# Differential attention's eight key tiles computed with layer 1's paired tiles, and all ten keys finished there

## The chip, the cores and the metric

The kernel runs on one core of one Trainium2 chip. The metric is the device time of one execution in microseconds (us). The engines are named as the profile names them: PE (TensorE, matmuls; PEld its weight loads), DVE (VectorE), ACT (ScalarE), POOL (GpSimd), SP (SyncE, which here only starts transfers). SBUF and PSUM are the on-chip memories; a "tile" below is a buffer in one of them, and a "column tile" is 128 output columns of a projection.

## The reference, cut to what matters

Two layers over 640 tokens: 512 latent ("sample") and 128 context ("prompt") tokens, 2048 wide. Layer 1 (the odd one) projects the normalised input with one matrix whose columns are split between differential attention (c) and grouped-query attention (d):

```python
p = h @ w_in                            # odd layer: cq, ck, cv, cg, dq, dk, dv, dg
cq = rms_norm(cq, cqn);  ck = rms_norm(ck, ckn)     # 2 maps x 4 heads of 128
q_d = rms_norm(q_d, dqn); k_d = rms_norm(k_d, dkn)  # 8 query heads, 2 key heads
new = (ck, cv, k_d, v_d)                            # context tokens: returned
cq, ck, q_d, k_d = (apply_rope(x, cos, sin) for x in ...)   # latent tokens
ck_all = concatenate([ctx[0], ck]);  cv_all = ...   # 256 cached + 512 latent keys
o1 = attend(cq[:, 0], ck_all[:, 0], cv_all)
o2 = attend(cq[:, 1], ck_all[:, 1], cv_all)
o_c = rms_norm(o1 - lam * o2, c_on) * (1.0 - lam_init)
y = concatenate([merge(o_c) * silu(cg), merge(o_d) * silu(dg)]) @ w_out
```

A key thus needs its projection, an RMS norm over 128 features, a gain, the axial rotation of the latent tokens, and, for the kernel's score products, a layout with the features on the partitions ("columns"). Every float32 product is made of three products of rounded parts (high x high, high x low, low x high); `split` (L296 to L298) makes the parts, the high one on ACT and the low one on DVE.

## The kernel before

**Two ways to project.** `run_tiles` (L388) makes one column tile at a time: 16 blocks of the contraction, 2 halves of 320 tokens, 3 products each, in four quarters of four blocks. Its weights are loaded five quarters ahead on SP's queue and split three quarters ahead. `run_pairs` (L533) makes two column tiles together with seven half-sized products, called M1, M5, M6, M2, M7, M3, M4 in this order, in place of eight (a scheme of Strassen's kind); each has 8 blocks and 3 products on 320 columns. Their operands are sums of weight blocks built on DVE (`operand`), and of the moving operand built beforehand (`forms`). The result of a column tile leaves in two halves through `done`: tile 0 after M2 and M3, tile 1 after M7 and M4.

**Slots.** After each quarter (`run_tiles`) or half product (`run_pairs`) a `slot` lets other work in: every generator of the list `prep` goes on by one yield, the list `attn` by a paced number of steps (`steps` per quarter, half of it between the two token halves), and a `fill` by a rate per quarter. In layer 1's attention stage the fill is `fill1` (L191): four blocks of the adaLN weights times the condition, two DVE products for each of 16 rows of a block, and a fold at its end; 68 steps in all, from the ninth quarter on (FILL1_FROM 8) at FILL1 0.85 a quarter. The tile framework that builds the program works out the waits, and it puts the instructions of each engine in order; this order is not always the written one.

**Layer 1's front** is `project` at L1715: gates, D's keys and all values. The first six column tiles run singly, the other twenty in ten pairs: four of gates, one of D's two keys (`dk`), one of D's values, four of C's. `gate_out` (L1652), `key_out` (L1678) and `value_out` (L1670) take the results out. A value is turned to rows there and stored (`value_rows`); a D key is only stored raw in `kdram` (L1684).

**Layer 1's attention stage** is the `run_tiles` at L1768: 26 single column tiles. First eight `dq` tiles; two of them start one grouped-query attention (`pair_gen`), whose keys are read back raw and finished by `k_gen` (L670) beside the first tile. Then for each of C's four heads two `cq` tiles and two `ck` tiles, then two late gates. For a `ck` tile `k_gen` copies the projection out of PSUM (`stage`), transposes it to rows (five PE transposes), sums the squares (ACT, L694), applies the gain (DVE, L696, L699), takes the power -0.5 (POOL, L704), scales (ACT, L707), rotates (DVE, L714 to L719), finishes the attention in hand (`drain(attn)`), transposes the two blocks of cached keys (L726) and the five blocks of the key back, and splits them into the tiles `k0h`, `k0l` or `k1h`, `k1l`, one buffer each. With the second key `diff_gen` (L1562) starts: 14 steps; a block's two maps go through one score tile `S` in PSUM, each by scores on PE (L847 to L849), the maximum on DVE (L809), its scaling and the exponential on ACT (L811, L816). Attention's pace is 1.6 steps a quarter up to the eleventh tile, then 1.1, and 1.75 in the late gates' tiles.

**What is loaded at the seam.** After the front SP issues the load of `tables` (rotation tables, 768 KB, L1718), then lambda, the output gains, and the cached and raw first key (L679, L684). Temporary tiles of the attention stage share few buffers: `rp` three, `stg` two.

Of the kernel before, what the change touches and what calls it, by code (L numbers as in the profile page):

```python
# [51 lines left out]
FILL1 = 0.85  # L52
# [4 lines left out]
def trunk_kernel(ctx: ExitStack, tc: tile.TileContext, I: dict, O: dict):  # L57
# [286 lines left out]
    prep, attn = [], []  # L344

# [324 lines left out]
    def k_gen(ap, pp, tag, src, gain, new_out, vals=None, then=None):  # L670

        vx = []

        def v_in(j):
            vx.append(ap.tile([P, 5, P], F32, tag="stg", name="vx", bufs=2))
            nc.sync.dma_start(vx[j].rearrange("p b f -> p (b f)"), vals[1][j])

        raw = ap.tile([P, 2, P], F32, tag="ctxk", name="ctxk", bufs=1)
        nc.sync.dma_start(raw, src.rearrange("(c p) d -> p c d", p=P))  # L679
        if isinstance(pp, tuple):  # L680
            x = stage(ap, pp)
        else:
            x = ap.tile([P, NT], F32, tag="stg", name="kx", bufs=2)
            nc.sync.dma_start(x, pp)  # L684
        if vals:
            v_in(0)
        yield
        ss = small.tile([P, 5], F32, tag="ss", name="ss")
        kg = ap.tile([P, 5, P], F32, tag="rp", name="kg", bufs=3)
        junk = ap.tile([P, P * st["sets"]], BF16, tag="junk", name="junk", bufs=1)[:, 0:P]  # L690
# [9 lines left out]
        if vals:  # L700
            v_in(1)
# [3 lines left out]
        yield  # L705
# [3 lines left out]
        m1 = ap.tile([P, 4, P], F32, tag="rp", name="m1", bufs=3)  # L709
        m2 = ap.tile([P, 4, P], F32, tag="rp", name="m2", bufs=3)  # L710
        x = kg[:, 0:4, :].rearrange("p b (a h f) -> p (b a) h f", a=2, h=2)
        y = m1.rearrange("p b (a h f) -> p (b a) h f", a=2, h=2)
        z = m2.rearrange("p b (a h f) -> p (b a) h f", a=2, h=2)
        V.tensor_mul(y, x, cosR[:, :, None, :].to_broadcast([P, 8, 2, 32]))  # L714
        yield
        V.scalar_tensor_tensor(out=z[:, :, 0, :], in0=x[:, :, 1, :], scalar=-1.0, in1=sinR,
                               op0=ALU.mult, op1=ALU.mult)
        V.tensor_mul(z[:, :, 1, :], x[:, :, 0, :], sinR)
        V.tensor_add(m1, m1, m2)  # L719
        yield  # L720
        drain(attn)
# [5 lines left out]
        split(hi[:, 0:CTX], lo[:, 0:CTX], t[:, 0:CTX])  # L727
        t = to_rows(lambda b: kg[:, b, :], False)
# [3 lines left out]
        if vals:  # L732
            yield
            hi, lo = st["v"] = tuple(ap.tile([P, 7, 2 * P], F32R, tag=t, name=t) for t in ("vh", "vl"))
            ctx_v(ap, vals[0], hi, lo, 2 * P)
            for j in range(2):
                cols = slice(j * P, (j + 1) * P)
                split(hi[:, 2:7, cols], lo[:, 2:7, cols], vx[j])
        if then:
            attn.append(then())  # L740
# [133 lines left out]
    def pair_gen(ap, width, k, v, qs, banded, begin, emit, done, sinks):  # L874
# [38 lines left out]
        for u in range(7):  # L913
# [8 lines left out]
            if u < 5:  # L922
                score(u, 1)
# [959 lines left out]
```

## Time and profile before

| what | value |
|---|---|
| runs shown | 2266.32 us median (2265.68 to 2266.66, 3 runs) |
| profiled execution | 2267.87 us, its span 2265.9 us |
| mean granted PE clock | 0.996 |
| layer 1's pairs | about 1190 to 1436 us |
| layer 1's attention stage | about 1436 to 2005 us |
| output projection of layer 1 | from about 2005 us |

The profile is one execution taken by the hardware profiler. Times in its rows count from the span's start; durations of groups are means in ns. "busy" of an engine is the time covered by its instructions. A group's row ends with the idle time of the engine just before these instructions and what ended it. Matmuls overlap, so their cost is read from the distance of their starts and not from their duration. SPq is SP's queue of transfers. L numbers are lines of the kernel before.

### The profile page before, as it was taken

What the parts mean: (1) busy time and instruction counts of PE and PEld (TensorE: products, weight loads), DVE (VectorE), ACT (ScalarE), POOL (GpSimd) and SP (SyncE); (2) the same over time, 40 slices, a digit from 0 to 9 for tenths busy, and PEclk for the clock granted to TensorE, in tenths of its full rate; (3) what the DMA queues carried; (4) which work ended last, traced back from release to release, by engine and by line L of the source; (5) the groups of instructions that cost most, each with busy time, mean ns of one, the idle gap of its engine ahead of it and who ended that gap; (6) DMA issues with size and microseconds to landing.
All of it is one profiled execution on the core that took longest, in us unless ns stands there. A gap on an engine that the chain in (4) does not pass through costs nothing.

```text
span 2265.9 us, 41110 instructions
## 1 busy us (share of the span) xinstructions
PE 2221.5 (98%) x15660; PEld 2148.4 (95%) x15660; DVE 1693.1 (75%) x2981; ACT 1167.9 (52%) x2473; POOL 223.5 (10%) x341
## 2 busy tenths in 40 slices
PE   7999999999999999999999999999999999999999
PEld 5889999999999999999999999899999999999999
DVE  4659898988888978877876666585766786576765
ACT  4335554645344445444744445577775666664443
POOL 2221101000100100000200000100001111111010
PEclk9999999999999999999999999999999999999999
DMA  9985556565453426753763333432424343246541
GB/s 357 330 287 173 160 167 198 173 188 161 154 156 113 150 85 219 218 148 106 261 200 108 117 110 112 151 103 70 124 84 140 96 132 111 83 134 224 166 135 45
DMA packets 377189, 354.03 MB, mean 156 GB/s; under 512 B 17170, under 2 KB 324848, under 8 KB 376480
## 3 DMA queue, kind: packets, MB, share of 16 engines
q1 hardware_dynamic: 360272, 291.07, 42.1%
q0 software_dynamic: 15856, 58.11, 7.3%
q8 instruction: 123, 2.02, 0.4%
q10 hardware_dynamic: 864, 2.23, 0.3%
q14 instruction: 74, 0.61, 0.1%
HBM read 307.17 MB, written 44.17 MB: 155 GB/s over the span
## 4 chain that ended last, share of the span: by engine, by line
PE 83%; DMA 4%; issue 4%; ACT 3%; DVE 3%; POOL 1%; SPq 1%; POOLq 0%; DVEq 0%; ACTq 0%
PE pq L626 10%; PE pq L628 10%; PE pq L627 10%; PE pa L332 6%; PE pa L333 6%; PE pb L332 6%; PE pa L334 6%; PE pb L333 6%; PE pb L334 6%; PE T L835 2%; PE S L847 2%; PE S L849 1%; PE S L848 1%; PE T L178 1%; DMA ada<-in_ada_w 1%
## 5 line engine op out<-in xcount | busy, mean ns | idle before, releaser
L297 ACT ACTIVATE wh<-raw 128x512 fp32r<-128x512 f32 (+1 forms) x388 | 233.2, 602 | 343.4 <-PE pb L333 227.4
L332 PE MATMUL pa<-h,wh 128*128 128x320 f32 x1152 | 367.7, 319 | 0.6 <-DVE sum L425 0.4
L332 PE MATMUL pb<-h,wh 128*128 128x320 f32 x1152 | 360.4, 313 | 0.9 <-ACT h L297 0.9
L333 PE MATMUL pa<-h,wh 128*128 128x320 f32 x1152 | 359.4, 312 | 0.9 <-DVE h L298 0.9
L334 PE MATMUL pa<-h,wl 128*128 128x320 f32 x1152 | 358.3, 311 | 0.0
L333 PE MATMUL pb<-h,wh 128*128 128x320 f32 x1152 | 357.8, 311 | 0.0
L334 PE MATMUL pb<-h,wl 128*128 128x320 f32 x1152 | 357.8, 311 | 0.0
L298 DVE TENSOR_TENSOR wl<-raw,wh 128x512 fp32r<-128x512 f32 (+1 forms) x388 | 253.5, 654 | 110.7 <-ACT wh L297 99.7
L626 PE MATMUL pq<-h,wh 128*128 128x320 f32 x960 | 297.7, 310 | 0.0
L627 PE MATMUL pq<-h,wh 128*128 128x320 f32 x960 | 296.6, 309 | 0.0
L628 PE MATMUL pq<-h,wl 128*128 128x320 f32 x960 | 296.4, 309 | 0.0
L332 PEld LDWEIGHTS pa<-h,wh 128*128 128x128 f32 x1152 | 217.4, 189 | 13.8 <-issue 12.5
L626 PE MATMUL pq<-T,wh 128*128 128x320 f32 x720 | 223.3, 310 | 0.0
L333 PEld LDWEIGHTS pa<-h,wh 128*128 128x128 f32 x1152 | 217.6, 189 | 5.9 <-issue 4.5
L628 PE MATMUL pq<-T,wl 128*128 128x320 f32 x720 | 222.6, 309 | 0.3 <-DVE wl L298 0.3
L627 PE MATMUL pq<-T,wh 128*128 128x320 f32 x720 | 222.4, 309 | 0.0
L332 PEld LDWEIGHTS pb<-h,wh 128*128 128x128 f32 x1152 | 217.2, 189 | 2.1 <-ACT h L297 1.1
L334 PEld LDWEIGHTS pa<-h,wl 128*128 128x128 f32 x1152 | 217.2, 189 | 2.1 <-issue 2.1
L333 PEld LDWEIGHTS pb<-h,wh 128*128 128x128 f32 x1152 | 217.5, 189 | 0.0
L334 PEld LDWEIGHTS pb<-h,wl 128*128 128x128 f32 x1152 | 217.2, 189 | 0.2 <-DVE wl L298 0.2
L297 ACT ACTIVATE wh<-sx 128x512 fp32r<-128x512 f32 x180 | 112.7, 632 | 154.5 <-PE pq L627 106.5
L251 DVE SCALAR_TENSOR_TENSOR acc<-adaw,sT,acc 128x1024 f32<-128x1024 f32 x150 | 189.3, 1278 | 0.0
(389 smaller groups left out, 4782.4 us busy)
## 6 DMA issues: line engine op xcount, KB each, us to landing
adaw<-in_ada_w SPq DMA_DIRECT2D x80, 512.0 KB, 3.9
raw<-in_od_w_in SPq DMA_DIRECT2D x148, 256.0 KB, 3.0
raw<-in_ev_w_in SPq DMA_DIRECT2D x130, 256.0 KB, 3.4
ada<-in_ada_w SPq DMA_DIRECT2D x11, 2048.0 KB, 12.7
adaw<-in_ada_w SPq DMA_DIRECT2D x64, 256.0 KB, 2.7
w<-in_od_w_in SPq DMA_DIRECT2D x30, 512.0 KB, 3.9
w<-in_ev_w_in SPq DMA_DIRECT2D x27, 512.0 KB, 3.7
adah<-in_ada_w SPq DMA_DIRECT2D x20, 512.0 KB, 9.2
```

Of the source, the lines that this page charges most:

```text
L178: PE.matmul(acc[32 * g:32 * g + 32, 0:wd], sT[:, kt, :], w[:, kt % m, :], start=(i < 4), stop=(i >= KT - 4), tile_position=(0, 32 * g))
L251: V.scalar_tensor_tensor(out=acc[c], in0=w, scalar=sT[:, kt, c:c + 1], in1=acc[c], op0=ALU.mult, op1=ALU.add)
L297: A.activation(hi, x, AF.Copy)
L298: V.tensor_sub(lo, x, hi)
L332: PE.matmul(ps, wh[:, i, :], hi[:, sl], start=(j == js[0] if alone else (pos == 0 and j == 0)), stop=False)
L333: PE.matmul(ps, wh[:, i, :], lo[:, sl], start=False, stop=False)
L334: PE.matmul(ps, wl[:, i, :], hi[:, sl], start=False, stop=(j == js[1] - 1 if alone else (pos == 3 and j == 3)))
L626: PE.matmul(ps, wh[:, j, :], hi, start=(first and h == 0 and j == 0), stop=False, skip_group_check=True)
L627: PE.matmul(ps, wh[:, j, :], lo, start=False, stop=False, skip_group_check=True)
L628: PE.matmul(ps, wl[:, j, :], hi, start=False, stop=(final and h == 1 and j == 3), skip_group_check=True)
L835: PE.transpose(t[:, i * P:(i + 1) * P], p, ident)
L847: PE.matmul(d, q[0][:, bs], k[0][:, ks], start=True, stop=False)
```

## The change

The eight `ck` column tiles leave the attention stage's list and join the front as four more pairs, behind the pair of D's keys and ahead of the values; the front has 14 pairs, and the attention stage 18 single tiles. All ten keys are finished in the front: a generator `key_chain` for each, with seven parts in the slots, makes the norm, gain and rotation and the transposes back, and stores the key as columns in `kdram` (ten entries now). The halves of the result go into the accumulator tiles `sq` and `acc`; `busy` holds back the next pair's results until the chain that reads the tile is through. The rotation tables for rows are loaded at the first pair into a part of `tables` that is free by then. In the attention stage a key is loaded as columns and only split, after the two transposes of the cached keys. In place of `drain(attn)` two counters (`passed`) tell when the attention in hand has made its last scores, or used its last values. A head's reload is a generator, `head_back`, started with its second query tile.

Sizes and rates: FILL1 0.85 becomes 1.1; steps are 1.6 a quarter up to the ninth tile and 2.0 after it, the late gates' tiles included; `rp` has two buffers in place of three, and a new tag `kk` has one. The first key's loads are issued ahead of the load of `tables`.

```diff
-FILL1 = 0.85
+FILL1 = 1.1
...
+    passed = {"scores": 0, "values": 0}
...
-    def k_gen(ap, pp, tag, src, gain, new_out, vals=None, then=None):
...
+    def key_rows(x, ss, kg, junk, gain):
+
         for sample in (True, False):
             t = to_rows(cols_of(x), sample)
             for i, b in enumerate(range(4) if sample else (4,)):
...
+        return r
+
+    def key_scale(kg, r, new_out, m1, cos):
+
         for b in range(5):
             A.activation(kg[:, b, :], kg[:, b, :], AF.Copy, scale=r[:, b:b + 1])
         nc.gpsimd.dma_start(new_out, kg[:, 4, :])
...
+    def key_turn(kg, m1, m2, sin):
...
+    def new_keys(ap, tag, raw):
+
         hi, lo = (ap.tile([P, 896], F32R, tag=tag + t, name=tag + t) for t in "hl")
         st[tag] = (hi, lo)
         t = psT()
         for c in range(2):
             PE.transpose(t[:, c * P:(c + 1) * P], raw[:, c, :], ident)
         split(hi[:, 0:CTX], lo[:, 0:CTX], t[:, 0:CTX])
+        return hi, lo
...
+            if u == 4:
+                passed["scores"] += 1
...
+    def key_chain(j, t):
+        yield
+        x, (gain, new_out) = st[t], KEYS[j][1:3]
+        ss = small.tile([P, 5], F32, tag="ss", name="ss")
+        kg = xr_tile("kg").rearrange("p (b f) -> p b f", b=5)
+        junk = pS.tile([P, 1024], F32, tag="S", name="sqj")[:, 0:P]
+        r = key_rows(x, ss, kg, junk, gains[gain])
+        yield
+        yield
+        m1 = x[:, 0:NS].rearrange("p (b f) -> p b f", b=4)
+        key_scale(kg, r, new_out, m1, cosF)
+        yield
+        m2 = xr_tile("m2")
+        key_turn(kg, m1, m2[:, 0:NS].rearrange("p (b f) -> p b f", b=4), sinF)
+        yield
+        yield
+        A.copy(m2[:, SPLIT], to_rows(lambda b: kg[:, b, :], False))
+        A.copy(m2[:, 0:NS], to_rows(lambda b: m1[:, b, :], True))
+        nc.gpsimd.dma_start(kdram[j], m2)
+        busy.discard(t)
...
     def key_out(j):
-        x = xr_tile("kx")
-
         def put(t, sl, src):
-            A.copy(x[:, sl], src)
+            A.copy(st[t][:, sl], src)
             if (j, "k") in half_done:
-                nc.gpsimd.dma_start(kdram[j], x)
+                busy.add(t)
+                prep.append(key_chain(j, t))
             half_done.add((j, "k"))
...
     def front_done(p, t, h, src):
-        outs[t](("sq", "acc")[t], HV[h][1], src)
+        tag = ("sq", "acc")[t]
+        while tag in busy:
+            advance(prep, len(prep))
+        outs[t](tag, HV[h][1], src)
...
-    nc.sync.dma_start(tables, I["k_tables"])
     close("mid")
     open_pool("odd")
+    st["sets"], st["rp"] = 2, 2
...
+    def key_load(j, tag, bufs):
+        ap = pools["cur"]
+        raw = ctx_keys(ap, KEYS[j][3])
+        x = ap.tile([P, NT], F32, tag=tag, name="kx", bufs=bufs)
+        nc.sync.dma_start(x, kdram[j])
+        return raw, x
+
+    def key_split(tag, raw, x):
+        hi, lo = new_keys(pools["cur"], tag, raw)
+        split(hi[:, CTX:], lo[:, CTX:], x)
+
+    first = key_load(0, "stg", 2)
+    nc.sync.dma_start(tables, I["k_tables"])
     odd_start()
...
+    def wait_for(what, n):
+        while passed[what] < n:
+            advance(attn, 1)
+
+    def head_back(h, n):
+        ap = pools["cur"]
+        k = key_load(2 + 2 * h, "kk", 1)
+        yield
+        yield
+        wait_for("scores", n)
+        key_split("k0", *k)
+        k = key_load(3 + 2 * h, "kk", 1)
+        craw = ap.tile([P, 2, 2 * P], F32, tag="ctxv", name="ctxv", bufs=1)
+        nc.sync.dma_start(craw, I["cache_c_v"][0, 0, h].rearrange("(c p) d -> p c d", p=P))
+        yield
+        key_split("k1", *k)
+        vx = [ap.tile([P, 5, P], F32, tag="stg", name="vx", bufs=2) for _ in range(2)]
+        for j in range(2):
+            nc.sync.dma_start(vx[j].rearrange("p b f -> p (b f)"), vdram[2 * h + j])
+        yield
+        wait_for("values", n)
+        hi, lo = st["v"] = tuple(ap.tile([P, 7, 2 * P], F32R, tag=t, name=t) for t in ("vh", "vl"))
+        split(hi[:, 0:2, :], lo[:, 0:2, :], craw)
+        for j in range(2):
+            cols = slice(j * P, (j + 1) * P)
+            split(hi[:, 2:7, cols], lo[:, 2:7, cols], vx[j])
+        attn.append(diff_then(h)())
...
     for h in range(4):
-        for m in range(2):
-            jobs.append((OD["cq"] + (m * 4 + h) * P, q_job(f"q{m}", "c_q_norm")))
-        for m in range(2):
-            more = (None, diff_then(h)) if m else ((I["cache_c_v"][0, 0, h], vdram[2 * h:2 * h + 2]),)
-            jobs.append((OD["ck"] + (m * 4 + h) * P,
-                         k_job(f"k{m}", I["cache_c_k"][0, 0, m, h], "c_k_norm", O["new_c_k"][0, 0, m, h], *more)))
-
-    brisk = {len(jobs): 1.75, len(jobs) + 1: 1.75}
-    brisk.update((i, 1.6 if i < 11 else 1.1) for i in range(2, len(jobs)))
+        jobs.append((OD["cq"] + h * P, q_job("q0", "c_q_norm")))
+        jobs.append((OD["cq"] + (4 + h) * P, last_q(h)))
+
+    brisk = {len(jobs): 2.0, len(jobs) + 1: 2.0}
+    brisk.update((i, 1.6 if i < 9 else 2.0) for i in range(2, len(jobs)))
```

More of the change, by code (lines that the diff above doesn't have):

```diff
@@ L752, in q_gen @@
         yield
[L753 removed]
+        m = ap.tile([P, NS], F32, tag="rp", name="qm", bufs=st["rp"])
         V.tensor_mul(m, x[:, 0:NS], cosT)
@@ new lines, in last_q, with f @@
+    def last_q(h):
+        def f(pp):
+            g = q_gen(pools["cur"], pp, "q1", gains["c_q_norm"])
+            next(g)
+            back = head_back(h, banded_before + 4 + h)
+            next(back)
+            prep.append(g)
+            prep.append(back)
+        return f
+    banded_before = passed["scores"]
+    for h in range(4):
+        jobs.append((OD["cq"] + h * P, q_job("q0", "c_q_norm")))
+        jobs.append((OD["cq"] + (4 + h) * P, last_q(h)))
+    brisk = {len(jobs): 2.0, len(jobs) + 1: 2.0}
```

121 lines of the change are left out of this document (59 added, 62 removed).

## The prediction

> **What bounds the kernel now.** I read the page first: engine totals, then the chain of work that ended last.
>
> ```profile
> PE 2221.5 (98%) x15660; PEld 2148.4 (95%) x15660; DVE 1693.1 (75%) x2981; ACT 1167.9 (52%) x2473; POOL 223.5 (10%) x341
> ...
> PE 83%; DMA 4%; issue 4%; ACT 3%; DVE 3%; POOL 1%; SPq 1%; POOLq 0%; DVEq 0%; ACTq 0%
> ```
>
> TensorE is the bound in total and on the chain, so a change in its work counts in full unless another engine takes its place. Totals hide stages, so next come the busy times by stretch: layer 1's pairs from 1190 to 1436 us, its attention stage from 1436 to 2005, and in it 200 us of differential attention. Columns: length, then PE, PEld, DVE, ACT, POOL, clock, DMA share, GB/s.
>
> ```profile
> 1190.00:1436.00 246.00, 246.00 (x1692) 245.77 (x1691) 159.64 (x235) 120.01 (x232) 16.16 (x30) 1.00 0.37 113
> 1436.00:2005.00 569.00, 557.23 (x3903) 533.43 (x3902) 390.60 (x739) 373.89 (x894) 65.04 (x91) 1.00 0.36 110
> 1700.00:1900.00 200.00, 196.50 (x1383) 188.79 (x1382) 151.44 (x293) 119.41 (x317) 27.93 (x45) 1.00 0.41 123
> ```
>
> In the pairs TensorE never stops, and VectorE is at 65%, ScalarE at 49%. In the attention stage TensorE stops for 2%. VectorE is at 69% there and at 76% in the differential part: it is the engine to watch.
>
> **The change part by part.**
>
> *Fewer products.* The duration of a matmul row (0.31 us) overlaps the next one, so I go by starts, in a pair and in a single tile.
>
> ```profile
> 1192.80 0.31 PE L627 MATMUL pq<-h,wh 128*128 128x320 f32 x1
> ...
> 1200.87 0.31 PE L628 MATMUL pq<-h,wl 128*128 128x320 f32 x1
> ...
> 1950.54 0.31 PE L332 MATMUL pb<-h,wh 128*128 128x320 f32 x1
> ...
> 1952.15 0.31 PE L334 MATMUL pb<-h,wl 128*128 128x320 f32 x1
> ```
>
> The first two are 55 steps apart (56 products): 8.07 / 55 = 0.1467 us. The last two are 11 apart: 0.1464. A single tile is 2 halves x 16 x 3 = 96 products, so two tiles are 192 and 28.2 us. A pair is 7 forms x 8 x 3 = 168 products and 24.6 us. Four pairs for eight tiles save 4 x 24 x 0.1467 = **14.1 us** of TensorE work, with no condition in the code on it. The ten transposes of each key stay as many; they move to the front with the chain. The two of the cached keys stay behind.
>
> *The start of the attention stage.* The waits of PE there, longest in total first (total, times, longest):
>
> ```profile
> PE S L847 <- ACT p L816: 2.3, 5, 0.6
> PE T L656 <- DMA kx<-kd: 2.2, 1, 2.2
> PE T L656 <- ACT kg L707: 1.5, 2, 1.1
> PE T L656 <- DVE k1l L298: 1.2, 1, 1.2
> ```
>
> and the clock just behind the second:
>
> ```profile
> 1444.00:1446.00 2.00, 0.65 (x4) 0.68 (x5) 0.80 (x4) 0.20 (x1) 0.00 (x0) 0.85 1.05 377
> 1446.00:1448.00 2.00, 2.00 (x9) 2.00 (x9) 0.36 (x1) 1.35 (x6) 0.00 (x0) 0.50 0.87 335
> 1448.00:1450.00 2.00, 2.00 (x13) 2.00 (x13) 1.50 (x4) 1.63 (x7) 0.68 (x2) 0.80 0.23 70
> ```
>
> The first D key comes back raw, behind the 768 KB of tables on SP's queue. Its transposes hold TensorE for 2.2 us, and the lost clock (0.15 + 0.50 + 0.20 of 2 us) is 1.7 us more. After, the key comes back as columns, ahead of the tables on that queue, and only the cached key's two transposes (128 KB) can hold TensorE; waits on the scaled key (1.5 us, L707) leave the stage. The gain lies between 0, if the cached key is as late as the raw one was, and 2.2 + 1.7 + 1.5 = 5.4. I take the middle, rounded down: **2.5 us**. [...]
>
> *The key chain in the front.* What a key costs VectorE and ScalarE (count | busy, mean ns):
>
> ```profile
> L714 DVE TENSOR_TENSOR m<-kg,tables 128x512 f32<-128x512 f32 x10 | 6.9, 693 | 18.9 <-ACT kg L707 18.9
> L696 DVE TENSOR_TENSOR kg<-T,gain_rows 128x512 f32<-128x512 f32 x10 | 6.9, 690 | 6.1 <-ACT junk L694 6.1
> L719 DVE TENSOR_TENSOR m<-m,m 128x512 f32<-128x512 f32 x10 | 6.9, 689 | 0.2
> ...
> L716 DVE SCALAR_TENSOR_TENSOR m<-kg,tables 128x256 f32<-128x256 f32 x10 | 4.2, 419 | 0.0
> L718 DVE TENSOR_TENSOR m<-kg,tables 128x256 f32<-128x256 f32 x10 | 4.2, 419 | 0.0
> ...
> L707 ACT ACTIVATE kg<-kg,r 128x128 f32<-128x128 f32 x50 | 15.9, 391 | 15.1 <-POOL r L704 15.1
> ...
> L694 ACT ACTIVATE junk<-T 128x128 bf16<-128x128 f32 x50 | 13.9, 277 | 2.9 <-PE T L656 1.7
> ...
> L694 ACT ACTIVATION_READ_ACCUMULATOR junk<-T 128x1 f32 x50 | 9.7, 195 | 0.0
> ```
>
> VectorE: 2.9 us in these rows, about 3.2 with the one product of 128 columns. ScalarE: 5 x (0.391 + 0.277 + 0.195) = 4.3 us, and about 0.9 for the two copies that gather the columns (an estimate by size from the same rows). A pair of keys adds 6.4 and 10.4 us of records. With 65% and 49% of 24.6 us as the base, less the gate's or the value's own work, VectorE comes to some 21 us and ScalarE to some 21 us of 24.6: near 85%. Each chain must end before its accumulator is written again ten slots of 1.76 us later (17.6 us); it needs, from its rows and with 1.2 us for POOL's power, about 12 us. Can a pair live with such a load? The nearest row is in layer 0's pairs:
>
> ```profile
> 740.00:780.00 40.00, 39.66 (x271) 39.40 (x270) 39.12 (x65) 16.76 (x29) 4.85 (x9) 1.00 0.48 146
> ```
>
> VectorE at 98% cost TensorE 0.3 us of 40. Five key pairs are 123 us, so that rate gives 1.0 us. ScalarE was low there, so both engines loaded at once isn't shown; the other end is a late chain, 3 us in each pair (17.6 against 12 and half as much again in queues), 15 us. I take **1 us**. POOL and SP's extra transfers (eight keys out and eight back, 320 KB each) lie beside a DMA share of 0.37.
>
> *A denser differential part.* This is the part that decides.
>
> ```profile
> L211 DVE SCALAR_TENSOR_TENSOR acc<-adaw,sT,acc 128x512 f32<-128x512 f32 x60 | 43.6, 745 | 2.7 <-DMA adaw<-in_ada_w 2.7
> L298 DVE TENSOR_TENSOR wl<-raw,wh 128x512 fp32r<-128x512 f32 x38 | 26.2, 689 | 14.8 <-ACT wh L297 12.1 <-PE T L656 2.2
> ```
>
> These rows are of 1700 to 1900 us: 38 quarter tiles in 200 us, so a head (16 quarters now) lasts 16 x 200 / 38 = 84 us, with 64 us of VectorE. After, a head has 8 quarters: 28.2 us less TensorE and 1.7 less for transposes, so 54 us. VectorE loses 8 splits (5.5 us), two key chains (6.4) and, since the adaLN fill runs at 1.1 rather than 0.85 a quarter on half the quarters, 18.9 - 13.1 = 5.8; records overlap by a tenth, so 16 of the 17.7. That leaves 48 us of 54: **88%, where it was 76%**. ScalarE falls to about 35 of 54. The fill still ends in time: 63 quarters x 1.1 = 69 steps for 68.
>
> The second pressure is latency: attention takes one step per half quarter (12 products, 1.76 us), and a head's two maps share the one score tile.
>
> ```profile
> 1950.36 0.34 PE L849 MATMUL S<-k0h,q0l 128*128 128x384 f32 x1
> ...
> 1950.74 0.96 DVE L809 TENSOR_REDUCE nm<-S 128x1 f32<-128x768 f32 x1 [1.72 <-PE S L849]
> ...
> 1952.06 0.99 ACT L816 ACTIVATE p<-S,nm,rq 128x768 f32<-128x768 f32 x1
> ```
>
> From the last score's step (1950.36 + 0.18) to the end of the exponential is 2.5 us. Now three or four half quarters' worth of products often lie between; after, 1.76 us do: 0.7 us short in 4 wide blocks of 4 heads, 11 us if nothing fills it. What can fill it are later products, which depend only on split weights. Bounds: **below**, the stage loses the share it loses now (3.5 of 200 us), and being 120 us shorter gives back 2.1; **above**, each of the 16 pairs of scores is also held by one pair of adaLN products ahead of the maximum (2 x 0.745): 16 x 2.2 = 35 us, less 2.1. The nearest row for full VectorE is
>
> ```profile
> 1836.00:1856.00 20.00, 20.00 (x138) 19.62 (x137) 19.74 (x37) 11.29 (x27) 2.29 (x3) 1.00 0.44 128
> 1856.00:1876.00 20.00, 19.72 (x143) 18.69 (x142) 18.71 (x35) 12.67 (x32) 2.77 (x5) 1.00 0.37 110
> ```
>
> VectorE at 96% for 40 us, TensorE 0.28 us idle. It speaks for the lower end, but it was a burst and the load after is steady, so I let half of the 11 us stand: 5.5 - 2.1, about **+3.4 us**.
>
> The queue of the waiting instruction: the keys' split waits on VectorE behind the maximum and the fill; behind it stand the weight splits, which are three quarters ahead (some 20 us with attention between), so TensorE feels it late. SP's reload of the second key waits for the first one's split, with weight loads behind it that are five quarters ahead. Both covers cost nothing while they last; gone, a weight load's landing (about 3 us by the page) is open each time.
>
> *Sum* against the profiled execution: span 2265.9 - 14.1 - 2.5 + 1.0 + 3.4 = 2253.7; with the 2.0 us around the span (2267.87 against 2265.9) 2255.7. The median of the runs stands 1.55 below the profiled execution, so **2254.1 us**.
>
> **The rivals.**
>
> *VectorE becomes the bound of the differential part (slower).* Place: between the two maps of each block. For it: 88% load, and a maximum that must pass the fill. [...] Against it: the 0.28 us of the burst above. It decides from the point where the other terms' 15.6 + 2.1 = 17.7 us are used up, 1.1 us a pair of scores. At its full price of 35 us the time is 2266.3 - 15.6 + 33 = 2283.7; at 1.4 us a pair it is 2271.
>
> *The front gives it back (no change).* The chains come late by 3 us in each of five pairs, because ScalarE and VectorE are near 85% at once and the next pair waits for the accumulator: 15 us for 1, so 2268. For it: nothing in the pairs loads both. Against: 17.6 us of room for 12.
>
> *All of it is gain (faster still).* The start gains 5.4, the front costs nothing and the differential part its lower bound: 2266.3 - 14.1 - 5.4 - 2.1 = 2244.7. For it: the burst rows. I count it with the forecast, at the low end.
>
> **How the numbers follow.** Runs of this kernel tell 0.2% (4.5 us) from no change. Forecast and its faster tail, below 2261.8: 0.68. The front, or a middling differential part, between 2261.8 and 2270.8: 0.13. VectorE as the bound, above: 0.19, of which over half ends below 2275. The range 2246 to 2275 leaves about 0.07 below and 0.09 above; the forecast's own is 2246 to 2261.
>
> **What would show it.** *Right:* 96 x 8 fewer products of single tiles and 672 more of pairs; the pairs' stage about 99 us longer with PE still near 100%; no wait of a transpose on `kx` and no half clock at the stage's start; a head of the differential part in 54 to 57 us with VectorE near 88%. *Wrong:* waits of the score products on the exponential (L847 on L816) growing from 2.3 us to over 15; idle PE in the key pairs, on `wl` or on a key's transposes; a new half-clock window at the start on the cached key's load; the fill unfinished when the stage ends, left for the output projection.

## The result and the profile after

| | before | after |
|---|---|---|
| median of the runs | 2266.49 us (2262.49 to 2269.07, 6 runs) | 2258.62 us (2256.06 to 2262.14, 6 runs) |
| ratio | | 0.9967, 95% interval 0.9956 to 0.9978 |
| profiled execution, its span | 2267.87, 2265.9 us | 2262.14, 2260.3 us |

The kernel became faster by 0.33%: 7.5 us, with an interval of 5 to 10. The forecast was 12.2 us less on the span, 2254.1 us for the median; the time lies inside its range. The direction was right, the size was not: about 60% of the gain came.

The page of the kernel after, engine totals and the chain that ended last:

```profile
PE 2212.2 (98%) x15564; PEld 2133.7 (94%) x15564; DVE 1728.9 (76%) x3027; ACT 1190.5 (53%) x2519; POOL 229.7 (10%) x349
...
PE 80%; ACT 6%; DMA 5%; DVE 4%; issue 4%; POOL 2%; SPq 0%; POOLq 0%; ACTq 0%; DVEq 0%
```

TensorE has 96 instructions fewer, the 4 x 24 products of the change. It is still the bound, with 3 points less of the chain. The totals can't say where the missing 40% went. So I cut the two traces at the same places, the first and the last projection products of a stage. PE's timeline of the kernel before (start, duration):

```profile
1180.78 0.31 PE L626 MATMUL pq<-h,wh 128*128 128x320 f32 x1
...
1431.87 0.31 PE L628 MATMUL pq<-T,wl 128*128 128x320 f32 x1
...
1432.02 0.31 PE L332 MATMUL pb<-h,wh 128*128 128x320 f32 x1
...
2131.45 0.31 PE L334 MATMUL pa<-h,wl 128*128 128x320 f32 x1
```

and of the kernel after:

```profile
1182.40 0.31 PE L627 MATMUL pq<-h,wh 128*128 128x320 f32 x1
...
1548.87 0.31 PE L629 MATMUL pq<-T,wl 128*128 128x320 f32 x1
...
1549.01 0.31 PE L332 MATMUL pb<-h,wh 128*128 128x320 f32 x1
...
2126.16 0.31 PE L334 MATMUL pa<-h,wl 128*128 128x320 f32 x1
```

The pairs take 366.5 us in place of 251.1 (+115.4), the single tiles behind them, 26 or 18 of the attention stage and the first 5 of the output projection, 577.1 in place of 699.4 (-122.3). Ahead of the pairs, in code that the change doesn't touch, the two executions differ by 1.6 us; over all fourteen profiled executions of this document the pairs start between 1178.8 and 1185.0 us. The single tiles are cut further at the starts of the third and of the ninth tile. Columns as in the prediction. Before:

```profile
1432.00:1471.30 39.30, 35.34 (x231) 32.88 (x230) 18.71 (x38) 21.75 (x64) 6.98 (x10) 0.96 0.57 183
...
1625.20:2131.50 506.30, 496.71 (x3469) 480.00 (x3468) 349.56 (x661) 299.60 (x724) 61.29 (x97) 1.00 0.42 129
```

After, with the pairs and a stretch of key pairs ahead of them:

```profile
1182.40:1548.90 366.50, 362.71 (x2499) 360.04 (x2498) 255.17 (x390) 204.75 (x490) 40.78 (x66) 1.00 0.35 107
...
1294.00:1434.00 140.00, 136.21 (x942) 133.58 (x942) 105.76 (x171) 93.39 (x275) 26.80 (x40) 1.00 0.32 99
...
1549.00:1579.60 30.60, 30.41 (x211) 29.38 (x210) 12.63 (x24) 15.03 (x32) 3.24 (x4) 1.00 0.75 240
...
1579.60:1734.70 155.10, 151.79 (x1068) 144.44 (x1067) 119.89 (x218) 113.81 (x231) 11.24 (x10) 1.00 0.37 114
...
1734.70:2126.20 391.50, 377.82 (x2621) 357.56 (x2620) 291.21 (x558) 247.54 (x548) 45.68 (x73) 1.00 0.46 144
```

The first two tiles became 8.7 us shorter: PE idles 0.2 us there, before it was 4.0, and the clock is 1.00 for 0.96. The pairs, which had no idle time, now have 3.8 us of it (366.50 - 362.71), all in the 140 us with the key chains. The stretch from the ninth tile on (C's heads, the late gates and the output projection's first tiles) is 114.8 us shorter, and its idle time rose from 9.6 to 13.7 us although it is shorter. The kernel before also loses 1.7 us there to a lower clock (0.63 and 0.52 of full speed from 2090 to 2094 us, in the output projection), the kernel after nothing.

To turn this into the terms of the forecast one more price is needed, that of the 100 transposes (ten for each key) which moved into the pairs. The first experiment gives it: without its stops the front is 360.6 us long, so 360.6 - 251.1 - 672 x 0.1467 = 10.9 us, 0.109 each. I take the same price for them in the attention stage, where none was measured; an error of 0.02 there would shift 2 us (0.02 x 100 transposes) between the terms.

| term | forecast | measured | how |
|---|---|---|---|
| fewer products | -14.1 | -14.1 | 96 fewer x 0.1467 |
| key chains in the front | +1.0 | +5.9 | 115.4 - 98.6 - 10.9 |
| start of the attention stage | -2.5 | -6.5 | -8.7, of it 20 moved transposes 2.2 |
| the rest of it and the output tiles | +3.4 | +7.8 | -113.6 + 768 x 0.1467 + 80 x 0.109 |
| sum | -12.2 | -6.9 | 115.4 - 122.3 |

All three small terms were too small, one with the gain and two with the loss. How well do such cuts repeat? The pairs do to 0.02 us in all executions of one code: 366.5 us in the three profiled kernels whose front is that of the change, 360.6 us in the seven with the first experiment's edit. The single tiles do not: the first experiment's kernel has the code of the change there and takes 575.1 us in place of 577.1, which makes the fourth term +5.3 in place of +7.8. And the profiled execution of the kernel after is the slowest of its six, 3.5 us above their median. So the fourth term is known as 5 to 8 us.

What TensorE waits for, total, times and longest, in the pairs of the kernel after:

```profile
PE T L657 <- DVE sq L703: 2.0, 5, 0.4
PE T L657 <- DVE acc L703: 1.8, 5, 0.4
```

and from the ninth single tile on, after:

```profile
PE S L846 <- ACT p L815: 3.8, 7, 0.8
PE T L657 <- DVE xr L1213: 2.2, 3, 1.7
PE T L1624 <- DVE on L1619: 2.2, 3, 0.7
```

and before, same stretch (the forecast's row, 2.3 us in 5 waits on the exponential, was of another stretch, 1436 to 2005 us):

```profile
PE S L847 <- ACT p L816: 2.4, 3, 1.6
...
PE T L1622 <- DVE on L1617: 0.9, 1, 0.9
```

Ten waits in the pairs, one for each key, are the clearest change. Behind the pairs nothing stands out: 1.4 us more on the exponential, 1.3 on the norm.

### The profile page after: what moved, and what is told of

Same layout as the page of the kernel before. It is cut to its first block, busy times and chain, and to the rows that moved or that the text cites. A ratio compares the mean times of both kernels' runs of the same rounds, so it can differ in the third digit from the quotient of the medians.

```text
span 2260.3 us, 41098 instructions
## 1 busy us (share of the span) xinstructions
PE 2212.2 (98%) x15564; PEld 2133.7 (94%) x15564; DVE 1728.9 (76%) x3027; ACT 1190.5 (53%) x2519; POOL 229.7 (10%) x349
## 4 chain that ended last, share of the span: by engine, by line
PE 80%; ACT 6%; DMA 5%; DVE 4%; issue 4%; POOL 2%; SPq 0%; POOLq 0%; ACTq 0%; DVEq 0%
PE pq L627 11%; PE pq L628 11%; PE pq L629 11%; PE pa L332 5%; PE pa L333 5%; PE pb L332 5%; PE pa L334 5%; PE pb L333 5%; PE pb L334 5%; PE T L834 2%; PE S L846 2%; DMA adaw<-in_ada_w 1%; PE S L848 1%; PE S L847 1%; PE T L178 1%
## 5 line engine op out<-in xcount | busy, mean ns | idle before, releaser
L627 PE MATMUL pq<-h,wh 128*128 128x320 f32 x1088 | 338.1, 311 | 0.0
L628 PE MATMUL pq<-h,wh 128*128 128x320 f32 x1088 | 336.2, 309 | 0.0
L629 PE MATMUL pq<-h,wl 128*128 128x320 f32 x1088 | 335.9, 309 | 0.0
L332 PE MATMUL pa<-h,wh 128*128 128x320 f32 x1024 | 325.2, 318 | 0.5 <-DVE sum L426 0.5
L332 PE MATMUL pb<-h,wh 128*128 128x320 f32 x1024 | 321.5, 315 | 0.9 <-ACT h L297 0.9
L333 PE MATMUL pa<-h,wh 128*128 128x320 f32 x1024 | 319.7, 312 | 0.2 <-DVE h L298 0.2
L333 PE MATMUL pb<-h,wh 128*128 128x320 f32 x1024 | 318.4, 311 | 0.0
L334 PE MATMUL pa<-h,wl 128*128 128x320 f32 x1024 | 317.6, 310 | 0.0
L298 DVE TENSOR_TENSOR wl<-raw,wh 128x512 fp32r<-128x512 f32 (+1 forms) x364 | 236.7, 651 | 87.9 <-ACT wh L297 83.9
L627 PE MATMUL pq<-T,wh 128*128 128x320 f32 x816 | 253.8, 311 | 0.0
L628 PE MATMUL pq<-T,wh 128*128 128x320 f32 x816 | 252.0, 309 | 0.0
L627 PEld LDWEIGHTS pq<-h,wh 128*128 128x128 f32 x1088 | 204.3, 188 | 0.8 <-issue 0.8
L332 PEld LDWEIGHTS pa<-h,wh 128*128 128x128 f32 x1024 | 192.5, 188 | 13.2 <-issue 12.2
L628 PEld LDWEIGHTS pq<-h,wh 128*128 128x128 f32 x1088 | 204.4, 188 | 0.0
L629 PEld LDWEIGHTS pq<-h,wl 128*128 128x128 f32 x1088 | 204.2, 188 | 0.0
L333 PEld LDWEIGHTS pa<-h,wh 128*128 128x128 f32 x1024 | 192.6, 188 | 5.9 <-issue 5.4
L332 PEld LDWEIGHTS pb<-h,wh 128*128 128x128 f32 x1024 | 193.5, 189 | 2.6 <-ACT h L297 1.1
```

Of the source, the lines that this page charges most:

```text
L298: V.tensor_sub(lo, x, hi)
L332: PE.matmul(ps, wh[:, i, :], hi[:, sl], start=(j == js[0] if alone else (pos == 0 and j == 0)), stop=False)
L333: PE.matmul(ps, wh[:, i, :], lo[:, sl], start=False, stop=False)
L334: PE.matmul(ps, wl[:, i, :], hi[:, sl], start=False, stop=(j == js[1] - 1 if alone else (pos == 3 and j == 3)))
L627: PE.matmul(ps, wh[:, j, :], hi, start=(first and h == 0 and j == 0), stop=False, skip_group_check=True)
L628: PE.matmul(ps, wh[:, j, :], lo, start=False, stop=False, skip_group_check=True)
```

## The experiments

Ratios are to the kernel before, run on the same chip; the change itself has 0.9967.

**The ten stops in the front.** What happens at one of them? PE in a key pair of the kernel after, with the idle time in brackets:

```profile
1341.60 0.31 PE L629 MATMUL pq<-h,wl 128*128 128x320 f32 x1
1341.75 0.27 PE L657 MATMUL T<-ident,kg 128*128 128x128 f32 x1
1342.40 0.66 PE L657 MATMUL T<-ident,sq 128*128 128x128 f32 x4 [0.38 <-DVE sq L703]
1342.81 0.39 PE L627 MATMUL pq<-T,wh 128*128 128x320 f32 x1
```

and VectorE at the same time:

```profile
1340.72 0.42 DVE L702 TENSOR_TENSOR m<-kg,tables 128x256 f32<-128x256 f32 x1
...
1341.06 0.68 DVE L298 TENSOR_TENSOR wl<-sx,wh 128x512 fp32r<-128x512 f32 x1
...
1341.66 0.68 DVE L703 TENSOR_TENSOR sq<-sq,m 128x512 f32<-128x512 f32 x1
```

The last transposes of a key stand in PE's order right behind a product that is done at about 1341.9. The sum that they read ends at 1342.34, because a weight split (L298) was put between the rotation's products (L702) and the sum (L703). All ten stops have this order on both engines, with 0.36 to 0.45 us idle. Either it is this distance of one slot, or the chain is late since VectorE is full. One more slot of distance tells them apart:

```diff
@@ key_chain, behind key_turn
         yield
+        yield
         A.copy(m2[:, SPLIT], to_rows(lambda b: kg[:, b, :], False))
```

> The changed kernel with one more yield between the rotation of a key and its last transposes, so the transposes come one half product (1.76 us) later. Theory A (the ten key chains lose about 0.6 us each because TensorE reaches the last four transposes 0.37 us before VectorE's last addition, which stands behind a weight split): the ten waits on that addition (3.8 us by the waits list) go, the five key pairs take 27.0 us each instead of 28.0, and the kernel gains 5 to 6 us against the changed one. Theory B (VectorE and ScalarE are too loaded in the key pairs, and the wait is only where it shows): the waits move to other instructions, the pairs stay at 28 us, gain under 2 us.

Measured: 2254.76 us, ratio 0.9943 (0.9929 to 0.9956), as theory A said. The pairs' first and last starts:

```profile
1183.04 0.31 PE L627 MATMUL pq<-h,wh 128*128 128x320 f32 x1
...
1543.60 0.31 PE L629 MATMUL pq<-T,wl 128*128 128x320 f32 x1
```

360.6 us for 366.5, and PE waits for nothing in the pairs. So 5.9 us hung on one yield. The ten waits were 3.8 us in the list; their removal gave 5.9, so a stop of 0.38 us costs 0.6. The rows agree: with the stop, the first transpose of the five starts 1.06 us ahead of the next product (1341.75 to 1342.81), without it 0.47 us (1342.90 to 1343.37 in this kernel). A full VectorE was not the cause: the weight split still stands ahead of the sum here, VectorE is busy 104.0 of the 135.0 us of the five key pairs (105.8 of 140 above), and TensorE has no idle time in them.

**VectorE's load in the attention stage.** The forecast expected the denser part to lose because VectorE comes to 88%. This kernel loads every row of the adaLN weights but multiplies two of 16 only (layer 1's adaLN gate is thus incomplete):

```diff
-                    else:
+                    elif kt == KT - 1:
                         V.scalar_tensor_tensor(out=acc[c], in0=w, ...
```

> The changed kernel with the adaLN fill of the attention stage reduced to its first and last row of weights per block (14 of 16 rows are loaded but not multiplied, so the adaLN gate of layer 1 is incomplete): 112 of the 128 VectorE products of 0.745 us are left out, 83 us of VectorE in 450 us. Theory C (the differential part's growth of lost time, from 13.7 to 18.9 us, comes from VectorE's load, 81% of that part): TensorE's lost time there falls below 12 us and the kernel gains 7 to 12 us. Theory D (it comes from the single score tile, whose release takes 2.5 us against 1.76 us of products): the waits of the scores on the exponential stay at about 6 us, gain under 4 us.

Measured: 2268.57 us, ratio 0.9997 (0.9986 to 1.0007): by the ratios 6.8 us slower than the change, where theory C had 7 to 12 us of gain. The third to eighth tile and the rest, to be read against the last two windows of the kernel after:

```profile
1578.00:1741.10 163.10, 155.20 (x1069) 147.09 (x1068) 87.88 (x165) 114.66 (x233) 11.22 (x10) 0.98 0.34 104
...
1741.10:2131.40 390.30, 379.20 (x2619) 361.07 (x2619) 256.05 (x497) 245.37 (x547) 45.96 (x73) 0.99 0.47 144
```

From the ninth tile on VectorE has 35 us less to do, and the stretch is 1.2 us shorter. Before it VectorE has 32 us less, and the stretch is 8.0 us longer: the framework built another order, with a wait on L909 that the kernel after hasn't there and longer ones on the exponential (after: 2.4 us, longest 0.9)

```profile
PE T L834 <- ACT p L909: 3.8, 2, 2.0
...
PE S L846 <- ACT p L815: 3.3, 3, 1.6
```

and with granted clocks of 0.98 and 0.99. From the ninth tile on TensorE's idle time is 11.1 us in place of 13.7, but its busy time is 1.4 us longer (379.20 for 377.82) at the clock of 0.99; over the whole execution the mean clock is 0.995, after 0.998. The kernel is thus no clean removal of load, and it doesn't settle what VectorE's load costs: 35 us less work came with 2.6 us less idle time, in another order.

**The pace of the attention's steps.** The change also raised `steps` to 2.0 from the tenth tile on (before: 1.1 from the twelfth). Here it is 1.75, with 2.0 left for the late gates:

```diff
-    brisk.update((i, 1.6 if i < 9 else 2.0) for i in range(2, len(jobs)))
+    brisk.update((i, 1.6 if i < 9 else 1.75) for i in range(2, len(jobs)))
```

> The changed kernel with 1.75 steps of attention a quarter in the differential part in place of 2.0 (14 steps a head, just enough). Theory C (VectorE's load): nothing changes in what VectorE does per head, within 2 us of the changed kernel. Theory D (the score tile's release against one half quarter of products): one half quarter in eight has no step, so some pairs of scores get 3.5 us; the waits of the scores fall from 6 to about 4 us and the kernel gains 2 to 4 us, unless more attention is left for the output projection's lead, where it costs some of it again.

Measured: 2259.07 us, ratio 0.9953 (0.994 to 0.9966). Theory D's 2 to 4 us came; the waits on the exponential fell by 1.5 us of them in the stretch below (2.3 us for 3.8). The front is as long as after (366.5), the single tiles are 570.9 us, 6.2 less. From the ninth tile on:

```profile
1735.50:2120.00 384.50, 376.08 (x2619) 357.37 (x2619) 291.20 (x557) 245.33 (x548) 46.17 (x73) 1.00 0.48 147
```

7 us shorter, with the same VectorE work; PE's idle time is 8.4 us for 13.7. With the loss of the kernel before and no more the stretch would be 506.3 - 112.7 - 8.7 = 384.9. Taken alone, these two traces would put the whole added loss there on the pace. But one is the slowest execution of its kernel and the other the fastest, and the runs show some 3 us against the change, with intervals that overlap; so it was repeated together with the first edit.

**Both edits together.**

> The changed kernel with both edits that helped alone: the later last transposes of a key and 1.75 steps a quarter in the differential part. Theory G (two separate losses, one in the front and one in the attention stage): the gains add, the front's pairs take 360.6 us and the single tiles behind them 571 us in the profile, 8 to 10 us less than the changed kernel, ratio to the kernel before near 0.993. Theory H (1.75 gained by chance of one order of instructions): the attention stage falls back to 575 to 577 us and the ratio stays at 0.994 to 0.995.

Measured: 2253.06 us, ratio 0.9933 (0.9921 to 0.9945), as theory G said; pairs 360.6, single tiles 573.7, which lies between the two theories. The same kernel on another chip:

> The kernel with both edits (later last transposes of a key, 1.75 steps), for comparison on one chip: near 0.993 of the kernel before, 5 to 7 us above the kernel with later norm transposes if that edit is worth what its first runs said, 0 to 2 us above it if it is worth what its profile said.

2249.99 us, ratio 0.9914 (0.9898 to 0.993), single tiles 572.4. From the ninth tile on, with the first edit alone

```profile
1730.20:2118.90 388.70, 377.12 (x2620) 357.46 (x2620) 291.17 (x557) 247.78 (x548) 46.01 (x73) 1.00 0.47 145
```

and with both (the second of the two runs):

```profile
1729.20:2115.20 386.00, 375.95 (x2621) 357.35 (x2620) 291.25 (x558) 245.18 (x548) 46.59 (x73) 1.00 0.48 146
```

Three profiles at 1.75 have 384.5, 385.1 and 386.0 us in this stretch, two at 2.0 have 391.5 and 388.7. That is 2.7 to 7 us in the traces and, twice, 0.1% in the runs (0.9967 to 0.9953, 0.9943 to 0.9933), each time inside the intervals: the direction agrees in all, the size is not settled. On both chips the kernel with both edits is faster than the change: 15 and 20 us under before.

**A slower pace still, and an earlier fill.** On both edits, 1.6 everywhere, and, as another kernel, the fill from the fifth quarter at 1.3:

```diff
+    brisk.update((i, 1.6) for i in range(2, len(jobs)))
...
+FILL1 = 1.3
+FILL1_FROM = 4
```

> The later transposes, and 1.6 steps a quarter for all of the attention stage up to the late gates (12.8 a head, where 14 are needed, so the reload of keys and values pushes the last step or two of each head through without products between). Theory D (the score tile's release against one half quarter of products): more pairs of scores have room, the waits of the scores on the exponential fall below 4.5 us, and the stage is no longer than with 1.75 (571 us). Rival (attention has to be spread over the whole stage): the pushed steps cost more than the room gives, the stage is back at 575 us or more.

> Both edits, and the adaLN fill at 1.3 steps a quarter from the fifth quarter on, so it ends after 56 quarters of 72 in place of 70, and the last two heads are free of it. Theory C (VectorE's load costs TensorE time): the grouped-query part gets dearer by about what the last heads gain, within 3 us of the kernel with both edits. Theory D (score tile and order): same, and the waits of the scores stay; a gain over 3 us would speak for C.

Measured: 2254.33 us, 0.9941 (0.9928 to 0.9955) at 1.6, with single tiles of 575.2, as the rival said, and 6.0 us of waits on the exponential, which theory D had below 4.5; no better than 1.75, so "slower is better" does not go on. The early fill: 2253.01 us, 0.9936 (0.9923 to 0.9949), single tiles 578.1, PE's waits on the exponential in the whole run 9.2 us (8, longest 2.7). Both theories allowed such a time; the stretches tell more. From the fifteenth tile on, with the fill over, VectorE has 147.1 us to do for 161.8 in the kernel with both edits, and the stretch is 215.5 us for 213.2 and 214.2: the lighter load gained nothing there. From the ninth to the twelfth tile the fill is denser, VectorE has 94.9 us for 88.2, and the stretch is 119.1 us for 115.0 and 114.9. So load is not shown to be the limit of the last heads, and a higher one is not shown to be free.

**The pace alone, in the kernel before.** (Here the late gates stay at 1.75.)

```diff
-    brisk.update((i, 1.6 if i < 11 else 1.1) for i in range(2, len(jobs)))
+    brisk.update((i, 1.6 if i < 11 else 2.0) for i in range(2, len(jobs)))
```

> The kernel before with 2.0 steps of attention a quarter in place of 1.1 from the twelfth tile on, keys where they were. VectorE's work per head is the same. Theory D (a step after each half quarter leaves the score tile 1.76 us for a release of 2.5): the scores' waits on the exponential grow from 3.9 us by 2 to 5 us, and the kernel gets slower by 2 to 6 us. Theory C (load): attention ends early in each head and products follow alone; within 2 us of the kernel before.

Measured: 2271.38 us, 1.0014 (1.0005 to 1.0023). A quick pace costs about 3 us where the tiles are sixteen and VectorE has room, too. But PE's waits on the exponential stayed (3.6 us in 7 waits, before 3.9 in 6, over all single tiles), those on the norm went from 0.9 to 2.4. So the trace doesn't show the forecast's mechanism, two maps that share one score tile, as what the pace costs here.

**The start of the stage by itself.** The kernel before with `key_chain` for D's two keys alone; C's keys stay in the attention stage, and no product is saved.

```diff
     def key_out(j):
...
-                nc.gpsimd.dma_start(kdram[j], x)
+                busy.add(t)
+                prep.append(key_chain(j, t))
...
     def keys_first():
-        for kv in range(2):
-            yield from k_job(f"k{kv}", I["cache_d_k"][0, 0, kv], ...)(kdram[kv])
+        key_split("k0", *first)
+        yield
+        second = key_load(1, "stg", 2)
+        yield
+        yield
+        key_split("k1", *second)
```

> The kernel before with one part of the change: only the two D keys are finished in the front (the chain, the columns, the first key's load ahead of the tables); C's eight key tiles stay in the attention stage, so not one product is saved. Theory I (the start of the attention stage gained because a key's chain left it): the stage's first two tiles take 30.5 us in place of 39.2, the half clock there goes, the one pair of keys takes 28 us in place of 24.7, sum about -5 us, ratio near 0.998. Theory J (the gain is that of the saved products, the rest cancels): what the start gains the pair gives back, ratio 1.000 within its interval.

Measured: 2263.89 us, 0.9983 (0.9974 to 0.9991): 2 to 6 us faster without one product less. The first two tiles:

```profile
1436.60:1467.40 30.80, 30.44 (x212) 29.41 (x211) 12.54 (x24) 15.36 (x32) 3.45 (x4) 1.00 0.73 230
```

30.8 us for 39.3, no half clock; the pairs are 254.5 us, 3.4 more than before, of which the 20 transposes are 2.2 and two stops 1.2. So this part of the change is worth about 5 us net in the trace and 4 in the runs: about half of the 7.5 us that the whole change gained.

**Why the start gained.** The forecast said that the first key waits behind the 768 KB of tables on SP's queue. In the kernel before, with the tables' load moved behind the first key's loads in the text:

```diff
-    nc.sync.dma_start(tables, I["k_tables"])
     close("mid")
...
     next(keys)
+    nc.sync.dma_start(tables, I["k_tables"])
```

> The kernel before, with the load of the rotation tables moved behind the loads of the first cached and raw key, and nothing else. Theory E (the start of the attention stage lost time because the first key came behind 768 KB of tables): the wait of the first transposes (2.2 us) and the half clock behind it (1.7 us) go, gain 3 to 4 us against the kernel before. Theory F (the key chain itself at the start costs it, whatever the order of the loads): the wait stays or turns into waits on the scaled key, gain under 1 us.

Measured: 2268.6 us, 1.0001 (0.9992 to 1.001), the waits as before. But SP's queue in its trace shows that the order did not change:

```profile
1432.37 0.34 SPq L1754 DMA_DIRECT2D tables<-in_k_tables  x1
1432.80 8.48 SPq L310 DMA_DIRECT2D raw<-in_od_w_in  x4
...
1442.35 0.43 SPq L679 DMA_DIRECT2D ctxk<-in_cache_d_k  x1
1442.88 0.89 SPq L684 DMA_DIRECT2D kx<-kd  x2
```

The tables still go first. So the run says nothing on them; it shows what else stands ahead of the key: four weight loads, which take the queue 8.48 us. In the kernel after each of the four is issued in 0.37 us, and between them the queue waits for weight splits (L298; 6.7 us in three waits). SP's queue in the kernel after, whose text has the key's loads ahead of the tables:

```profile
1546.15 0.34 SPq L1776 DMA_DIRECT2D tables<-in_k_tables  x1
1546.58 8.48 SPq L310 DMA_DIRECT2D raw<-in_od_w_in  x4
1555.11 0.50 SPq L707 DMA_DIRECT2D ctxk<-in_cache_d_k  x1
1555.66 0.46 SPq L1768 DMA_DIRECT2D kx<-kd  x1
```

There, too, the framework kept the tables in front, and the same four weight loads; and so in the kernel with D's keys alone (tables at 1433.76, key at 1443.29). The key's load is issued 6.7 us into the stage (first product at 1549.01); in the kernel above it was 7.7 (1435.23). What reads it (rows of the key's tile: duration in ns min/median/max, first and last start):

```profile
L297 ACT ACTIVATE k0h<-kx x5: 727/731/741, 1560.5 to 1976.9; 128x640 fp32r<-128x640 f32 x5
L298 DVE TENSOR_TENSOR k0l<-kx,k0h x5: 805/817/826, 1561.3 to 1980.8; 128x640 fp32r<-128x640 f32 x5
```

ACT and VectorE, for the split; no transpose on TensorE reads it any more, and the only stop that is left there is 0.2 us on the cached key. The key still comes late: ACT waits 1.7 us for it and starts at 1560.5, when TensorE has long passed the cached key's transposes (1557.95); the first score reads the split key at 1589.4. The wait went because TensorE no longer reads the late tile; that the tile comes 1.8 us earlier in the stage (11.5 us for 13.3) would not have been enough.

**The norm of the differential part.** On both edits, the products with the values one block earlier than the output's transposes, to give the norm more time; run twice, the second time beside the repeat of both edits above.

```diff
         for u in range(8):
-            if u >= 3:
-                out(u - 3)
             if 2 <= u < 7:
                 weigh(u - 2)
+            if u >= 3:
+                out(u - 3)
```

> The kernel with both edits, and in a step of differential attention the transposes of the normed block put behind the weighing of the next one (2.2 us later on TensorE). Theory K (what the differential part still loses is waits of single instructions put a little too early in TensorE's order): the waits of these transposes on the norm (3.0 us) go and the kernel gains 2 to 3 us against the one with both edits. Theory D (the score tile decides): TensorE comes to the score sooner and waits there instead; the waits of the scores grow by what the others lose, gain under 1 us.

> The kernel with later norm transposes once more, now on the same chip as the kernel with both edits. The first time it was 0.30% below that kernel by the runs, while the profile showed about 1 us less in the stage where the edit acts. If the runs were right, the two differ by 5 to 7 us again; if the profile was, by 0 to 2 us.

Measured: 2246.65 us, 0.9903 (0.9888 to 0.9918), and 2248.93 us, 0.9912 (0.9897 to 0.9928), beside 0.9914 for the same kernel without the edit on the second chip. The norm's waits (3.0 us) went, and others came: over the single tiles 6.5 us on the exponential for 5.2, 1.2 on the low parts of the softmax weights (L1605) for none. The edit makes no difference that was measured; without the repeat it would have passed for 0.3%.

## Why the prediction came out as it did

The time fell in the range partly by luck: the start gained 4.0 us more than forecast, and the other two small terms lost 7 to 9 us more.

**Fewer products, -14.1: right.** 96 instructions fewer, at the step that the rows of before gave.

**Start of the stage, -2.5 between 0 and 5.4: right in kind, above the upper end.** The step that failed is "I take the middle, rounded down". The idle time went from 4.0 to 0.2 us and the half clock (1.7 us) went, 5.5 together; the balance above has 6.5. The lower end was "the cached key as late as the raw one"; it waited 0.2 us. The reason given, the key ahead of the tables on the queue, falls: the queue of the kernel after still has the tables first. What held was that TensorE would read the cached key alone.

**The key chain in the front, +1 between 0 and 15: the step that failed most clearly.** It was priced by load and by the chain's length (12 of 17.6 us). Both were harmless: VectorE had the 21 us a pair that were forecast, ScalarE 19 for 21, in a pair of 28.0 us and not 24.6 (76% and 67%); with one more slot the same work left TensorE no idle time, and no accumulator was late. What cost 5.9 us is the order in which the last link of a chain meets TensorE: transposes one slot behind a VectorE sum that a weight split delays. It is the forecast's own sign, "idle PE on a key's transposes". The experiment with one more slot shows it. (The sign "pairs about 99 us longer" left out the 10.9 us of the transposes that move there; with them it is 109.5, and 115.4 were measured.)

**A denser differential part, +3.4: right in direction, half the size or a little more, and the reason isn't shown.** From 1794 to 2030 us, the eight tiles in which four heads are worked off, VectorE has 192.0 us: the forecast's 48 a head. But a head takes 59 us, not 54 to 57, so the share is 81% and not 88%. Part of this is a misreading: the 84 us of before, from which the 54 came, are 86.3 by the starts of tiles (three heads from 1724.5 to 1983.3 us), so a head without added loss is 56. Part is work that moved: the five tiles of the output projection behind take 96.3 us, before 102.2. That VectorE's load is the cause was not borne out: without the fill the last tiles were no shorter; nor is it excluded, since the light kernel had another order and a denser fill went with a longer stretch. The waits on the exponential rose to 3.8 us and not to over 15, so the short distance of the two maps is no large term, and the rival "VectorE becomes the bound" fell.

What moves this term in the traces is the pace of 2.0, which the forecast had read only as the time between two steps: at 1.75 the same work leaves 8.4 to 10.0 us idle for 11.6 to 13.7. Open is which dependence the pace strains: no single wait shrinks by that much, PE's busy time shrinks by 1.2 to 1.9 us as well, and the runs bear out 2 to 3 us of the 2.7 to 7, inside their intervals.

**The rivals.** "The front gives it back" had the right place and the wrong mechanism, at 5.9 of its 15 us. "All of it is gain" was right for the start alone.

## What to carry to other kernels

A chain that moves beside a bound engine is to be priced link by link where that engine reads it: ask what stands right ahead of the reading instruction, and what its producer stands behind; a load of 76% said nothing on that here, and one slot of distance is a cheap test. Where a wait is removed, ask whether the late tile comes sooner or the bound engine stops reading it; here the second took the idle time of the first two tiles from 4.0 to 0.2 us, with a tile that still came late. And a change with a sure saving may earn its gain elsewhere: here about half came from a part that saves no product, and two small edits around it (one slot, one pace) were worth as much again.

## What the runs showed of the hardware

A wait of 2.5 us was again followed by half clock, as the one of 2.2 us in the kernel before: in the kernel with the tables moved,

```profile
1446.00:1448.00 2.00, 0.33 (x3) 0.07 (x1) 1.18 (x5) 0.20 (x1) 0.00 (x0) 1.00 0.94 327
1448.00:1450.00 2.00, 1.12 (x6) 1.16 (x7) 0.00 (x0) 0.16 (x1) 0.00 (x0) 0.76 1.04 374
1450.00:1452.00 2.00, 2.00 (x10) 2.00 (x9) 0.69 (x1) 1.77 (x9) 0.00 (x0) 0.50 0.43 164
1452.00:1454.00 2.00, 2.00 (x14) 2.00 (x14) 1.72 (x3) 1.05 (x4) 1.29 (x2) 0.88 0.36 96
```

the clock column lacks 0.24 + 0.50 + 0.12 of 2 us, 1.7 us. The change and the kernel with D's keys alone, which don't have this wait, have a clock of 1.00 over the first two tiles. The runs don't show what length of a wait brings the half clock. The waits at this place are 2.2 and 2.5 us long. But in the kernel before no product starts for 3.5 us (1442.82 to 1446.28), since the five transposes stand behind the wait, and the rows don't show which of the two lengths the half clock goes with. Nor is length all: in the kernel with later norm transposes a wait of 1.69 us (to 1707.66, first run) was followed by half clock, its products 0.27 us apart in place of 0.147 from 1708.94 to 1711.87; the wait at the same place in the second run was longer, 2.00 us (to 1708.58), and the products behind it are 0.146 us apart. So half clock can follow a wait of this size and need not. Where the clock column was read it cost 1.7 us each time: at two places of the kernel before, 1444 to 1450 and 2090 to 2094 us, and in the rows above.

A stop of 0.38 us between products cost 0.6 us, not 0.38: ten of them 5.9 us. And the same kernel gave 0.9933 and 0.9914 of the kernel before on two chips, with intervals that overlap: a difference as large as some edits above, so an edit of that size was compared beside its rival on one chip.
